# Values of the forgetting heads: three chunks of 344 columns, or two of 512 with half of K in block products

## The chip, the cores and the metric

The kernel runs on one core of one Trainium2 chip. The core's engines each work through a list of instructions of their own: TensorE (PE in the profile, with its weight loads as PEld), VectorE (DVE), ScalarE (ACT), GpSimd (POOL) and SyncE (SP), the last two used here mostly to issue transfers (DMA). The metric is the device time of one execution in microseconds; lower is better.

## The reference

One layer: RMSNorm, one wide projection, two groups of eight attention heads (128 wide), an output projection, and a convolutional feed-forward part, over 256 tokens of width 2048 in float32.

```python
h = rms_norm(x, attn_norm)
proj = h @ w_in                       # 2048 x (3*1024 + 8 + 3*1024)
qa, ka, va, fa, qb, kb, vb = split(proj)
qa, ka = rms_norm(to_heads(qa), q_norm), rms_norm(to_heads(ka), k_norm)
c = cumsum(log_sigmoid(fa + b_forget))         # fa: one column per head, 8 in all
out_a = softmax(qa @ ka.T / sqrt(128) + c[t] - c[s], s <= t) @ va
out_b = stick_breaking(qb, kb, vb)
x = x + concat(rms_norm(out_a), rms_norm(out_b)) @ w_out
x = x + conv_ffn(rms_norm(x))
```

The change concerns `va` (1024 columns) and `fa` (8 columns): `h @ w_in[:, 2048:3080]`.

## The kernel before

**Numbers in two parts.** Each float32 operand of a large product is split into a high part of the type fp32r and the rest, also fp32r: for a weight tile, ScalarE casts (`act.copy`, L220) and VectorE subtracts (L221), both in `split`. A product is then three matmuls: high by high, low tokens by high weights, high tokens by low weights (`in_three`, L237). The tokens `hT` are kept transposed, 16 K tiles of 128 features, each with both parts and 256 tokens; a matmul takes a 128x128 piece of `hT` as the stationary operand and streams the weights' columns.

**A slab.** `token_major` (L253) computes both token tiles for up to 512 columns: for each four K tiles it loads the weights (`load`, three raw buffers), splits them (two buffers each for the high and low parts), and issues 4 x 3 x 2 = 24 matmuls into `acc` (two PSUM banks). After each such slab it calls `step()`, which advances the generators that stand waiting (rows to be normed and transposed, gates, heads), and takes one step of a generator `behind`.

**Order.** The program runs an opening (the first 512 query columns) whose order is written out by hand; behind it PE's order is that of the program and the other engines' order comes from a planner, in which loads and splits have a raised priority. Then come the forgetting heads' values and gates (L558 to L568), the keys' first half, the queries' second half, the keys' second half, the other group, the output projection, and the feed-forward part.

**The values.** Three chunks of 344 columns, 1032 in all, hold the 1024 value columns and the 8 forget columns behind them. `values` scales them by `rstd1` into three tiles: token tile 0 as high and low part, token tile 1 whole.

**Queries and keys.** `fox_rows` (L332) scales a chunk into `raw`, squares it and sums the squares per head on VectorE, takes the root (`rsqrt`, L108: ScalarE's Ln and Exp between short VectorE operations), and multiplies; some steps later it transposes the rows (`ps_h`).

**Block products.** In the output projection half of the columns over half of K already go by a scheme of seven block products in place of eight (`in_seven`, L835): tokens and weights are taken as 2x2 blocks, the tokens' sums are made on VectorE (`block_sums`, `block_parts`), and the weights' sums in place, one on VectorE (`w += x12`) and the others by transfers that add into SBUF on POOL's queue (`plus`). Each product is 12 matmuls of 512 columns into one PSUM bank, and VectorE adds the bank to its targets after each. Products into the same bank accumulate. The scheme's steps are taken by `token_major`, one behind each slab. `pg` (L920), four one-column products, stands in the same stage.

**A transfer near the change.** As soon as `rstd1` is there, POOL writes it to DRAM element by element (`row`, L689) and reads it back as `R1`.

Of the kernel before, what the change touches and what calls it, by code (L numbers as in the profile page):

```python
# [15 lines left out]
P = 128  # L16
D = 2048
S = 256
# [28 lines left out]
def hybrid_layer(  # L47
# [59 lines left out]

    def rsqrt(out_, ss, scale, n):  # L108
# [5 lines left out]
        act.activation(y, y, AF.Exp, scale=-0.5)  # L114
# [3 lines left out]
        dve.tensor_tensor(out_, y, u, op=ALU.mult)  # L118
# [13 lines left out]
    hT = [None] * KT  # L132

    def new_tokens(g):
        t = big.tile([P, 4, 2, S], F32R, name=f"hT{g}", tag=f"hT{g}")
        hT[4 * g : 4 * g + 4] = [t[:, i] for i in range(4)]

# [67 lines left out]
    def load(src):  # L205
        raw = wraw.tile([P, 2048], F32, name="w_raw", tag="w_raw")
        a, b = src.shape[1:]
        nc.sync.dma_start(raw[:, : a * b].rearrange("p (a b) -> p a b", a=a), src)
        return raw

    in_turn, last_split = [], []

    def split(raw, a, b):
        hi = whi.tile([P, 2048], F32R, name="w_hi", tag="w_hi")
        lo = wlo.tile([P, 2048], F32R, name="w_lo", tag="w_lo")
        n = a * b
        with ExitStack() as turn:
            for ins in in_turn:
                turn.enter_context(tc.issue_after(ins.ins))
            last = [act.copy(hi[:, :n], raw[:, :n])]  # L220
            last.append(dve.tensor_tensor(lo[:, :n], raw[:, :n], f32(hi[:, :n]), op=ALU.subtract))  # L221
        last_split[:] = last
        if in_turn:
            in_turn[:] = last
# [79 lines left out]
    with ExitStack() as actx:  # L304
# [9 lines left out]
        def project(c0, cols):  # L314
            return token_major(lambda k: hT[k], wi, 0, KT, c0, cols)
# [15 lines left out]

        def fox_rows(acc, dst, g, steps=2):  # L332
# [6 lines left out]
            for t in range(NT):  # L339
# [3 lines left out]
                dve.tensor_tensor(sq, raw, raw, op=ALU.mult)  # L343
                ss = small.tile([P, 4], F32, name="ss", tag="ss")
                dve.tensor_reduce(ss, sq.rearrange("p (h d) -> p h d", h=4), axis=AX.X, op=ALU.add)
                r = small.tile([P, 4], F32, name="r", tag="r")
                rsqrt(r, ss, 1.0 / HD, 4)
                dve.tensor_tensor(r3, r3, r.unsqueeze(2).to_broadcast([P, 4, HD]), op=ALU.mult)
# [8 lines left out]
        oT_fox = late.tile([P, NH, 2, S], F32R, name="oT_fox")  # L357
        oT = [oT_fox[:, h] for h in range(NH)]
# [4 lines left out]
        def attended(po, h, g, group):  # L363

            if len(done) == NH:
# [175 lines left out]

        qT0 = fox_queries(0)
        waiting.append(fox_rows(acc_q0, qT0, gq, 4))
        step()


        vA_parts = at.tile([P, 2, WF], F32R, name="vA", tag="vA")
        vA = (vA_parts[:, 0], vA_parts[:, 1], vA_rest)
# [8 lines left out]

        lf = at.tile([P, NT, NH], F32, name="lf")  # L558
# [17 lines left out]
        def gates():  # L576
# [4 lines left out]
            act.activation(la, la, AF.Ln, bias=1.0)  # L581
            dve.scalar_tensor_tensor(lf, lf, 0.0, la, op0=ALU.min, op1=ALU.subtract)
# [87 lines left out]
        for half in range(2):  # L670
            if half:
                qT = fox_queries(1)
                waiting.append(fox_rows(project(512, 512), qT, gq, 3))
# [4 lines left out]
            waiting.append(fox_rows(project(WF + 512 * half, 512), kT, g_k))  # L678
# [99 lines left out]
        in_order = tc.keep_in_program_order  # L778
        blocks, sums = [], []

        def block_sums():

            for h, tag in enumerate(("minus_c1", "blocks")):
                blocks.append(at.tile([P, 4, S], F32, name=f"oT_blocks{h}", tag=tag))
# [517 lines left out]
```

## Time and profile before

| | |
|---|---|
| median of 3 runs | 1100.91 us (1100.86 to 1101.10) |
| profiled execution, its own time | 1100.61 us |
| its span, first to last instruction | 1098.8 us |
| granted TensorE clock | 1.000 |
| PE instructions | 5856 matmuls |
| DMA over the span | 249.04 MB, mean 227 GB/s |
| first value slab to first slab of the keys | 31.83 to 78 us |

How to read the lines. The chain of waits in order of time has, for each piece, its start (us), its length (us), the engine, the tile written, the line and the number of instructions. Groups of instructions have the line, engine and operation, output and inputs with their shapes, the count, busy time and the mean of one (ns), and the idle time ahead with what ended it. A window has its bounds and length, then busy time with the count for PE, PEld, DVE, ACT and POOL, the granted clock, the DMA engines' share, and GB/s. Lines on a tile give the shortest, median and longest duration in ns. Lines on transfers have the queue, the count, the size and the median time to landing in us. A wait has who waited for whom, the total in us, how often, and the longest.

### The profile page before, as it was taken

How to read it: one execution, taken by the hardware profiler on the slowest of the kernel's cores; microseconds unless marked ns; L12 is line 12 of the kernel's file. 1: busy time of each engine (PE TensorE's matmuls, PEld its weight loads, DVE VectorE, ACT ScalarE, POOL GpSimd, SP SyncE). 2: the span in 40 equal slices, each digit the busy share in tenths (PEclk: the TensorE clock that was granted, in tenths of full speed). 3: DMA queues.
4: the chain of work that ended last, by engine and by line, in shares of the span. 5: the costliest groups of instructions: out<-in, count | busy, mean ns of one | idle time of the engine just before them, and what ended most of it. 6: DMA issues, size and time to landing. Idle time of an engine off the chain costs nothing.

```text
span 1098.8 us, 14833 instructions
## 1 busy us (share of the span) xinstructions
PE 1094.2 (100%) x5856; PEld 949.3 (86%) x5856; DVE 895.2 (81%) x957; ACT 709.3 (65%) x884; POOL 47.9 (4%) x49
## 2 busy tenths in 40 slices
PE   9999999999999999999999999999999999999998
PEld 7998888888888888888888888888888888888887
DVE  5755777977789776789889988799798889889896
ACT  6544556664665566767757776777676677677753
POOL 0000000000000000001010000100000010100010
PEclk9999999999999999999999999999999999999999
DMA  8776654576639395558999597977979688987985
GB/s 289 183 235 230 190 155 153 192 231 195 226 118 284 110 333 195 168 180 229 278 233 292 191 251 262 259 262 183 320 203 308 211 222 276 248 264 196 324 205 180
DMA packets 180991, 249.04 MB, mean 227 GB/s; under 512 B 4480, under 2 KB 119066, under 8 KB 180666
## 3 DMA queue, kind: packets, MB, share of 16 engines
q1 hardware_dynamic: 162458, 209.67, 58.3%
q0 software_dynamic: 18144, 37.89, 18.4%
q8 instruction: 46, 0.75, 0.3%
q10 hardware_dynamic: 320, 0.53, 0.1%
q14 instruction: 23, 0.19, 0.0%
HBM read 245.97 MB, written 2.11 MB: 226 GB/s over the span
## 4 chain that ended last, share of the span: by engine, by line
PE 100%; ACT 0%; DVE 0%; issue 0%
PE pu L271 34%; PE acc L245 20%; PE pu L277 18%; PE bank_a L245 11%; PE bank_b L245 5%; PE bank_c L245 3%; PE acc L446 2%; PE acc L1180 1%; PE ps_x L146 1%; PE ps_o L612 1%; PE bank_a L1180 1%; PE ps_p L628 0%; PE ps_o L613 0%; PE ps_h L324 0%; PE idle L399 0%; PE ps_s L540 0%
## 5 line engine op out<-in xcount | busy, mean ns | idle before, releaser
L221 DVE TENSOR_TENSOR w_lo<-w_raw,w_hi 128x2048 fp32r<-128x2048 f32 (+1 forms) x194 | 434.9, 2245 | 119.9 <-ACT w_hi L220 119.2
L220 ACT CAST w_hi<-w_raw 128x2048 fp32r<-128x2048 f32 (+1 forms) x194 | 363.6, 1876 | 221.8 <-PE acc L245 61.2
L271 PE MATMUL pu<-hT,w_hi 128*128 128x512 f32 x1664 | 394.0, 390 | 0.0
L271 PEld LDWEIGHTS pu<-hT,w_hi 128*128 128x128 f32 x1664 | 310.3, 188 | 63.1
L277 PEld LDWEIGHTS pu<-hT,w_lo 128*128 128x128 f32 x1664 | 211.9, 191 | 7.0
L277 PE MATMUL pu<-hT,w_lo 128*128 128x256 f32 x1664 | 215.1, 283 | 0.0
L245 PE MATMUL acc<-w_hi,hT 128*128 128x512 f32 (+1 forms) x576 | 124.4, 368 | 0.0
L245 PEld LDWEIGHTS acc<-w_hi,hT 128*128 128x128 f32 x576 | 101.6, 188 | 14.5
L221 DVE TENSOR_TENSOR w_lo<-w_sum,w_hi 128x2048 fp32r<-128x2048 f32 x34 | 77.9, 2290 | 23.1 <-ACT w_hi L220 23.1
L220 ACT CAST w_hi<-w_sum 128x2048 fp32r<-128x2048 f32 x34 | 64.9, 1910 | 46.6 <-PE pu L271 36.4
L997 ACT ACTIVATE tap<-up,ccol 128x256 f32<-128x256 f32 x176 | 74.6, 495 | 0.0
L245 PE MATMUL acc<-w_lo,hT 128*128 128x512 f32 (+1 forms) x288 | 64.6, 366 | 0.0
L245 PEld LDWEIGHTS acc<-w_lo,hT 128*128 128x128 f32 x288 | 51.6, 188 | 7.5
L1102 POOL DMA_DIRECT2D w_sum<-in_w_down_dram x20 | 25.4, 1272 | 678.5 <-DVE w_lo L221 665.4
L245 PE MATMUL bank_a<-w_hi,g 128*128 128x512 f32 x160 | 40.0, 392 | 0.0
L245 PE MATMUL bank_b<-w_hi,s 128*128 128x512 f32 x160 | 40.0, 392 | 0.0
L245 PE MATMUL bank_a<-w_hi,s 128*128 128x512 f32 x160 | 40.0, 392 | 0.0
L245 PEld LDWEIGHTS bank_a<-w_hi,g 128*128 128x128 f32 x160 | 28.9, 189 | 5.3
L245 PEld LDWEIGHTS bank_a<-w_hi,s 128*128 128x128 f32 x160 | 28.9, 189 | 5.3
L245 PEld LDWEIGHTS bank_b<-w_hi,s 128*128 128x128 f32 x160 | 28.9, 189 | 5.3
L1002 DVE TENSOR_TENSOR gate<-gate,tap 128x512 f32<-128x512 f32 x44 | 30.3, 689 | 2.5 <-ACT tap L997 0.2
L1002 DVE TENSOR_TENSOR val<-val,tap 128x512 f32<-128x512 f32 x44 | 30.3, 688 | 2.3
(248 smaller groups left out, 1107.5 us busy)
## 6 DMA issues: line engine op xcount, KB each, us to landing
w_raw<-in_w_up_dram SPq DMA_DIRECT2D x88, 1024.0 KB, 7.6
w_raw<-in_w_down_dram SPq DMA_DIRECT2D x44, 1024.0 KB, 6.0
w_raw<-in_w_in_dram SPq DMA_DIRECT2D x36, 1024.0 KB, 5.5
w_sum<-in_w_down_dram POOLq DMA_DIRECT2D x20, 1024.0 KB, 10.1
w_raw<-in_w_out_dram SPq DMA_DIRECT2D x14, 1024.0 KB, 6.7
w_raw<-in_w_down_dram POOLq DMA_DIRECT2D x10, 1024.0 KB, 14.8
w_raw<-in_w_in_dram SPq DMA_DIRECT2D x12, 688.0 KB, 4.2
w_raw<-in_w_in_dram SPq DMA_DIRECT2D x6, 512.0 KB, 7.0
```

The costliest lines, as they stand in the source:

```text
L146: nc.tensor.transpose(ps[:, j, t * P : (t + 1) * P], xt[t][:, (k + j) * P : (k + j + 1) * P], ident)
L220: last = [act.copy(hi[:, :n], raw[:, :n])]
L221: last.append(dve.tensor_tensor(lo[:, :n], raw[:, :n], f32(hi[:, :n]), op=ALU.subtract))
L245: nc.tensor.matmul(o, lhs(i, l, t), r[:, i, :], start=starts and j == 0, stop=stops and j == 3 * n - 1, skip_group_check=more,)
L271: nc.tensor.matmul(acc[:, j, :], hi[:, i, j * P : (j + 1) * P], hT[k].rearrange("p a b -> p (a b)"), start=k == 0, stop=low_first and k == ...
L277: nc.tensor.matmul(acc[:, j, S:], lo[:, i, j * P : (j + 1) * P], hT[k][:, 0, :], start=False, stop=not low_first and k == KT - 1,)
L446: nc.tensor.matmul(acc[:, t, :], of_half(hT[2 * c + i + j], l, t), r[:, j, :], start=high and c == i == m == 0, stop=not high and c == 7 a ...
L612: nc.tensor.matmul(po, v[j][:, hs], wp[:, k], start=i == 0, stop=False)
L997: act.activation(taps[w][:, j, :], u[:, j, w : w + S], AF.Copy, scale=ccol[:, w, f : f + 1])
L1002: dve.tensor_tensor(a, a, tap, op=ALU.add)
L1102: nc.gpsimd.dma_start(mem[into][:, : nk * 512].rearrange("p (a b) -> p a b", a=nk), src, accum_op=ALU.add)
L1180: nc.tensor.matmul(o, of_half(g, l, t), r[:, i, c0 : c0 + cols], start=kh == 0 and j == 0, stop=kh == n - 1 and j == 11,)
```

## The change

The values become two chunks of 512 columns. For K tiles 8 to 15 they are computed plainly, four slabs. For K tiles 0 to 7 the product is taken by the seven block products, whose code is generalised from the output projection's and used by both; its steps run behind the slabs of the values (one product behind each slab of the second chunk), of the keys' first half and of the queries' second half. The token sums come from `hT`. Each product's bank is added on VectorE, scaled by plus or minus `rstd1`, into four tiles of 512 columns; when all are done, token tile 0 is split into high and low part.

The 8 forget columns are loaded apart (`wg_raw`, 2048 rows of 32 bytes) and multiplied by 64 matmuls: for each K tile and token tile one of 16 columns (high tokens by both weight parts) and one of 8 (low tokens by high weights).

In `fox_rows`, ScalarE squares and sums, head by head, in place of VectorE's product and reduction. The first queries' rows wait three steps in place of four. The splits from the values to the queries' second half are issued in turn, and some behind named instructions (`last_split`): root, squares, rows, gates. `x12`, one tile in the output projection, is two half tiles here. `oT_fox` is allocated when the first head is done, in the buffer that held the token sums.

```diff
 def fox_rows(acc, dst, g, steps=2):
...
-                dve.tensor_tensor(sq, raw, raw, op=ALU.mult)
                 ss = small.tile([P, 4], F32, name="ss", tag="ss")
-                dve.tensor_reduce(ss, sq.rearrange("p (h d) -> p h d", h=4), axis=AX.X, op=ALU.add)
+                for h in range(4):
+                    some = slice(h * HD, (h + 1) * HD)
+                    squared = act.activation(sq[:, some], raw[:, some], AF.Square, accum_out=ss[:, h : h + 1])
+                squares_done.append(squared)
...
+        def in_seven(src, of_tile, sums, w, x12, add, places, idle_steps, prepared, at_once):
+
+            w11, w12, w21, w22 = src
...
+            def product(bank, lhs, parts, to, minus=False):
+                new = bank not in banks
+                if new:
+                    pool, tag = places[bank]
+                    banks[bank] = pool.tile([P, 512], F32, name=bank, tag=tag)
+                in_three([banks[bank]], parts, 4, lhs, new, True, more=not new)
+                add(*to, banks[bank], minus)
...
+            for _ in range(idle_steps):
+                yield
+            if not at_once:
+                first_loads(moved, (w, w11))
+            product("bank_a", of_blocks(0, 0), prepared(lambda: split(w, 4, 512), sum_weights), (0, 0))
+            if not at_once:
+                yield
+                first_loads(moved_x12, (w12,))
+            product("bank_c", of_blocks(1, 0), weights(w21, 4, 512), (0, 0))
+            yield
+            if not at_once:
+                last_split.append(gates_done[0])
+                with tc.issue_after(gates_done[-1].ins):
+                    sum_weights()
+                yield
+                last_split.extend(gates_done)
+            parts = split_ahead(w)
+            moved(nc.gpsimd, w, w22, accum_op=ALU.add)
+            moved_x12(nc.gpsimd, w22, accum_op=ALU.add)
+            product("bank_b", of_sums(0, 1), parts, (1, 1))
+            yield
+            product("bank_b", of_sums(1, 0), weights(w22, 4, 512), (0, 1))
+            yield
+            parts = split_ahead(w)
+            moved(nc.gpsimd, w, w21, accum_op=ALU.add)
+            product("bank_a", of_sums(1, 1), parts, (0, 1), True)
+            yield
+            product("bank_a", of_sums(0, 0), split_ahead(x12), (1, 1), True)
+            yield
+            product("bank_a", of_blocks(1, 1), split_ahead(w), (1, 0))
...
+        def values_in_seven():
+
+            sums = late.tile([P, 2, NH, S], F32R, name="hT_sums", tag="eight")
+            last_split.append(rooted_done[0][1])
+            with tc.issue_after(rows_done[-1].ins):
+                block_parts(block_sums(hT_of_four[:2]), [sums[:, part] for part in range(2)])
+
+            def add(t, h, ps, minus=False):
+                some = value_columns[t][h]
+                factor = (minus_rstd1 if minus else rstd1)[:, t : t + 1]
+                dve.scalar_tensor_tensor(some, ps, factor, some, op0=ALU.mult, op1=ALU.add)
...
+        nc.sync.dma_start(wg_raw, rows_of(wi, 0, KT, 3 * WF, NH))
+        act.copy(wg[:, :, 0, :], wg_raw)
+        dve.tensor_tensor(wg[:, :, 1, :], wg_raw, f32(wg[:, :, 0, :]), op=ALU.subtract)
+        ordered[0] = True
+        last_split.clear()
+        seven = values_in_seven()
+        for h in range(2):
+            if h:
+                last_split.append(squares_done[-1])
+            acc = token_major(lambda k: hT[8 + k], wi, 8, 8, 2 * WF + 512 * h, 512, seven)
+            for t in range(NT):
+                scaled(value_columns[t][h], acc[:, t, :], t)
+
         lf = at.tile([P, NT, NH], F32, name="lf")
-        for j in range(3):
-            acc = project(2 * WF + 344 * j, 344)
-            n = 344 if j < 2 else 336
+        pf = psb.tile([P, NT, 2, NH], F32, name="pf", tag="t")
+        for k in range(KT):
             for t in range(NT):
-                if j == 2:
-                    dve.scalar_tensor_tensor(
-                        lf[:, t, :], acc[:, t, 336:344], rstd1[:, t : t + 1], bf,
-                        op0=ALU.mult, op1=ALU.add,
-                    )
-            values([v[:, 344 * j : 344 * j + n] for v in vA], acc[:, :, :n])
+                nc.tensor.matmul(
+                    pf[:, t].rearrange("p a h -> p (a h)"), of_half(hT[k], 0, t),
+                    wg[:, k].rearrange("p a h -> p (a h)"), start=k == t == 0, stop=False,
+                )
+                nc.tensor.matmul(
+                    pf[:, t, 0, :], of_half(hT[k], 1, t), wg[:, k, 0, :], start=False, stop=k == KT - 1 and t == NT - 1,
+                )
...
-                waiting.append(fox_rows(project(512, 512), qT, gq, 3))
+                waiting.append(fox_rows(project(512, 512, seven), qT, gq, 3))
+                ordered[0] = False
...
-            waiting.append(fox_rows(project(WF + 512 * half, 512), kT, g_k))
+            waiting.append(fox_rows(project(WF + 512 * half, 512, seven), kT, g_k))
```

More of the change, by code (lines that the diff above doesn't have):

```diff
@@ L353, in fox_rows @@
             yield
-        oT_fox = late.tile([P, NH, 2, S], F32R, name="oT_fox")
-        oT = [oT_fox[:, h] for h in range(NH)]
+        oT, oT_fox = [], []
         vA_rest = late.tile([P, WF], F32, name="vA_rest", tag="two_heads")
@@ L363, in attended @@
         def attended(po, h, g, group):
+            if not done:
+                oT_fox.append(late.tile([P, NH, 2, S], F32R, name="oT_fox", tag="eight"))
+                oT.extend(oT_fox[0][:, h] for h in range(NH))
             if len(done) == NH:
```

226 lines of the change are left out of this document (127 added, 99 removed).

## The prediction

> **What bounds the kernel now.** I read the page first, then what TensorE (PE) waited for, then the chain of waits in order of time around the values, then the same chain around the output projection, where the block scheme already runs.
>
> ```profile
> PE 1094.2 (100%) x5856; PEld 949.3 (86%) x5856; DVE 895.2 (81%) x957; ACT 709.3 (65%) x884; POOL 47.9 (4%) x49
> PE 100%; ACT 0%; DVE 0%; issue 0%
> ...
> PE idle L399 <- DVE zeros L389: 1.1, 1, 1.1
> PE acc L446 <- ACT hT L151: 0.3, 1, 0.3
> ```
>
> PE is busy over the whole span, the chain is all PE, and in the whole run it waited twice, for 1.4 us, both at the start. So the time is the sum of PE's instructions. An edit gains what it takes from PE, loses what it adds there, and everything on the other engines is free until PE has to wait for it.
>
> ```profile
> 31.83 15.12 PE acc L245 x96
> 46.95 0.87 PE ps_h L324 x8
> 47.82 35.73 PE acc L245 x216
> ...
> 83.76 5.47 PE acc L245 x24
> ```
>
> The values are 3 chunks of 344 columns by four slabs (a slab is one load of weights, four K tiles) of 24 matmuls, 288 in all. The first four slabs (x96) take 15.12 us, 3.78 each. The 216 matmuls behind them hold eight such slabs and the first slab of the keys (5.47, as its successor): (35.73 - 5.47) / 8 = 3.78. **Removed from PE: 12 x 3.78 = 45.4 us.**
>
> **What takes its place on PE.** Two kinds are shown at full size by the output projection:
>
> ```profile
> 307.22 5.44 PE acc L245 x24
> 312.66 0.34 PE pg L920 x4
> 313.00 5.61 PE acc L245 x24
> ...
> 325.92 2.75 PE bank_a L245 x12
> 328.67 2.72 PE bank_c L245 x12
> ```
>
> The second half of K, plain: 2 chunks x 2 slabs = 4 slabs of 24 matmuls of 512 columns, 4 x 5.44 = 21.8 us. The first half of K: seven products of 12 matmuls, 7 x 2.73 = 19.1 us. Together 40.9 us, that is 4.5 less than was removed (the columns streamed fall from 288 x 344 = 99,072 to 180 x 512 = 92,160).
>
> The third kind is new: 16 K tiles x 2 token tiles x 2 parts = 64 matmuls that stream 16 or 8 columns, each with its own 128x128 stationary tile of `hT`. The streaming is nearly nothing; each still needs its weight load. The nearest rows are the four one-column products `pg`, which also load a full 128x128 tile each:
>
> ```profile
> L920 PEld LDWEIGHTS pg<-cs,ssq x8: 187/190/192, 312.3 to 347.8; 128*128 128x128 f32 x8
> L920 PE MATMUL pg<-cs,ssq x8: 164/250/250, 312.5 to 347.8; 128*128 128x1 f32 x8
> ...
> L245 PEld LDWEIGHTS acc<-w_hi,hT 128*128 128x128 f32 x576 | 101.6, 188 | 14.5
> ```
>
> On the chain four of them cost 0.34 us, 0.085 each; but the slab behind them takes 5.61 in place of 5.44, since its first load is exposed too: (0.34 + 0.17) / 4 = 0.128 each. These are my bounds: 64 x 0.085 = 5.4 and 64 x 0.128 = 8.2 us. In a run of 64 the ends (one load hidden before, one exposed behind) count for little, so I take the value between, 0.110: **64 x 0.110 = 7.0 us added**. A load is 188 ns long for tiles of `hT` and 190 for `ssq`; that the type (fp32r here, fp32 in `pg`) makes it cheaper is not to be seen; 344- or 512-column products hide such a load behind the product before, 16 columns hide none of it.
>
> The Trainium skill speaks against that price: "TensorE: Matmul & The Clock Gate", section "Back-to-back issue gap", gives a floor of about 25 ns for matmuls of 1 to 64 columns; that is the first rival below. The same page, "LDWEIGHTS (loading the stationary operand)", gives columns / 1.2 ns, 107 ns for 128; the trace agrees with that one (0.085 to 0.128).
>
> Sum on PE: -45.4 + 21.8 + 19.1 + 7.0 = **+2.5 us**; with the bounds +0.9 to +3.7. Against the profiled execution's 1100.61 us this is 1103.1; the median of the runs shown is 0.3 above that execution, so 1103.4.
>
> **What is added beside PE, costed at nothing.** These five windows reach from the first value slab to the second slab of the next queries:
>
> ```profile
> 31.80:47.60 15.80, 15.80 (x106) 15.78 (x104) 11.39 (x24) 6.56 (x12) 1.84 (x3) 1.00 0.79 151
> 47.60:62.80 15.20, 15.20 (x100) 15.20 (x98) 7.57 (x6) 8.50 (x9) 0.00 (x0) 1.00 0.83 251
> 62.80:77.90 15.10, 15.10 (x98) 15.10 (x98) 7.56 (x5) 6.83 (x7) 0.00 (x0) 1.00 0.75 249
> 77.90:99.70 21.80, 21.80 (x98) 17.66 (x98) 10.78 (x10) 9.31 (x11) 1.59 (x3) 1.00 0.74 242
> 99.70:122.70 23.00, 23.00 (x112) 19.28 (x111) 17.55 (x30) 10.69 (x16) 0.00 (x0) 1.00 0.60 193
> ...
> L221 DVE TENSOR_TENSOR w_lo<-w_raw,w_hi 128x2048 fp32r<-128x2048 f32 x10 | 22.9, 2292 | 17.4 <-ACT w_hi L220 17.4
> L221 DVE TENSOR_TENSOR w_lo<-w_raw,w_hi 128x1376 fp32r<-128x1376 f32 x12 | 19.1, 1590 | 15.9 <-ACT w_hi L220 15.9
> L343 DVE TENSOR_TENSOR sq<-raw 128x512 f32<-128x512 f32 x4 | 2.6, 686 | 0.0
> L345 DVE TENSOR_REDUCE ss<-sq 128x4 f32<-128x512 f32 x4 | 2.5, 680 | 0.0
> ...
> L786 DVE TENSOR_TENSOR oT_blocks<-oT_fox 128x1024 f32<-128x1024 f32 x2 | 2.4, 1220 | 0.0
> L833 DVE SCALAR_TENSOR_TENSOR x<-bank_b,rg,x 128x512 f32<-128x512 f32 x2 | 1.5, 750 | 0.3 <-PE bank_b L245 0.3
> ...
> w_sum<-in_w_out_dram POOLq DMA_DIRECT2D x2, 1024.0 KB, 10.4
> ```
>
> VectorE (the third number after the span) is busy 54.9 of 90.9 us there. Twelve splits of 1.59 go (-19.1), eleven of 2.29 come (+25.2: four plain, seven for the products); the weights' sum 2.3, block sums (2 x 1.22 and four of about 0.69) 5.2, their low parts 2.4, seven bank reads of 0.75 5.3; squares and reductions leave for ScalarE (-5.1); the values' own low parts about even. That is 71 of 93.4 us, 76%: it fits, and so does ScalarE by the like sum (41.9 to some 59 us, squares included). The cover is the same slab of PE work that hides a split today: two splits (4.6 us on VectorE) against a slab and a product (5.44 + 2.72 = 8.2). Without it a split costs its 2.29 us on PE. The chain of three in-place sums of `w` through POOL's queue, 10.4 us to land in the output projection (last row above), has 11 us and more between the split before and the product behind; `minus_c`'s transfers stand in that queue too, but are short. Three waits are new on the queues: the third slab's cast on ScalarE stands behind the eight squares, `w_11`'s behind the queries' root, the sum of weights on VectorE behind the gates. PE is the only one that waits for these splits. The new `wg_raw` load waits for no buffer, so on SP it can go ahead of the second value slab's weights, which do.
>
> **Rivals.**
>
> *The small products are cheap* (ends faster).
>
> ```profile
> 312.50 0.28 PE L920 MATMUL pg<-cs,ssq 128*128 128x1 f32 x2
> ```
>
> The first two `pg` take 0.28 us together and the second 0.25 by itself (its median above): it starts 0.03 us behind the first, so its load was done ahead. If every load of `hT` could overlap its neighbour like that, the 64 would cost 64 x 0.03 = 1.9 us: 1100.6 - 4.5 + 1.9 = 1098.0. It decides from 4.5 / 64 = 70 ns down. Against it: the four `pg` together average 85, so the third and fourth had to wait for their loads. The Trainium skill's floor, above, would be an estimated 64 x 0.025 = 1.6 us here and 1097.7.
>
> *A transfer comes late at the start* (slower still).
>
> ```profile
> 26.50:30.00 3.50, 3.50 (x16) 2.64 (x15) 2.50 (x5) 3.50 (x6) 0.00 (x0) 1.00 0.00 0
> 37.50:46.00 8.50, 8.50 (x56) 8.50 (x56) 7.48 (x18) 3.24 (x6) 0.54 (x1) 1.00 0.67 29
> 46.00:52.00 6.00, 6.00 (x42) 5.98 (x42) 2.08 (x3) 3.46 (x6) 0.00 (x0) 1.00 0.97 311
> ACT w_hi L220: 5.3, 1
> DMA to landing us min/median/max: 4.2/4.5/11.1
> DMA packets 308, 0.15 MB, mean 128 GB/s; under 512 B 171, under 2 KB 308, under 8 KB 308
> ```
>
> Each window's last number is GB/s: from 37.5 to 46.0 us the transfers move 29 while `rstd1` is written to DRAM element by element; a slab's load took 11.1 us and ScalarE waited 5.3 us for it, without reaching PE. After the change, PE wants the first product's cast (`w_11`) at 31.8 + 3 x 5.44 = 48.2, so its load by 46.3; the fourth slab by 49.0, `w_21` by 54.4. Ahead of these the queue has two slabs a third larger, and `wg_raw`: 2048 packets of 32 bytes, 128 an engine. In the window where the forget bias's 128 packets of that size pass (22.2 to 23.4), 308 packets take 1.2 us, 62 ns each on an engine: 8 us for `wg_raw`, of which the 3.5 us without a transfer before 30.0 us cover less than half. If `w_11` has all its 1 MB left at 46.0, it lands at 49.4 (3.4 us at 311 GB/s) and PE waits 3.1 us; the fourth slab and `w_21`, each 3.4 us behind the one before, add 0.7 and 1.4: 5.2 in all, 1108.3. With half of it left, about half: 1106. By my count PE's loads just make it.
>
> *The third slab's cast is late.*
>
> ```profile
> 35.62 1.26 ACT L318 ACTIVATE raw<-acc,rstd 128x512 f32<-128x512 f32 x2
> ...
> L658 ACT ACTIVATE pr<-pr,nm 128x128 f32<-128x128 f32 x1 | 0.4, 402 | 4.2 <-DVE nm L655 4.2
> L658 ACT ACTIVATION_READ_ACCUMULATOR pr<-pr,nm 128x1 f32 x1 | 0.2, 187 | 0.0
> L220 ACT CAST w_hi<-w_raw 128x2048 fp32r<-128x2048 f32 x10 | 19.1, 1912 | 21.6 <-PE acc L245 21.5
> ```
>
> `raw` is scaled by 36.9 us, or 0.9 sooner now that the third cast (34.4 to 35.7 before) goes behind it. Eight squares of 128 columns take at most 8 x 0.59 (0.40 + 0.19, as this accumulating activation), to 40.7; the cast of 1.91 ends at 42.6, and PE wants it at 31.8 + 2 x 5.44 = 42.7. A slip of 1 us gives 1104.4.
>
> **How the numbers follow.** Forecast, no new wait on PE and small products at 0.110 us: 0.55, 1103.4. Late transfer: 0.20, 1106. Late cast: 0.13, 1104.4. Cheap small products: 0.07, 1098.0 to 1100. Something else: 0.05. The range 1101.5 to 1107.5 runs from the lower bound of the small products (+0.9) to most of the late transfer. What can be told from no change is 0.2%, 2.2 us: the forecast lies only just beyond it, and a small product of 0.105 us or less falls back into it, so of its 0.55 some 0.09 count as the same. Slower 0.83, same 0.10, faster 0.07.
>
> **What would show it.** Four plain slabs at 5.44 and seven products at 2.72 on the chain; one piece of 64 small matmuls, 7.0 us long, between the last `bank_c` and the keys; PE's waits still those two. Wrong if that piece is below 4.5 us, or if PE waits for `w_hi` between 42 and 57 us by more than 1 us.

## The result, and the profile after

The changed kernel takes 1112.79 us, median of 5 executions (1111.2 to 1114.0), against 1101.1 (1100.86 to 1102.04) for the kernel before: a ratio of 1.0104 with a 95% interval of 1.0089 to 1.0118. The sign was forecast, the size was not: the 11.7 us are nearly five times the 2.5 of the forecast, and the time lies beyond its range of 1101.5 to 1107.5. The profiled execution took 1114.0 us, 13.4 more than that of before, its span is 1112.2 us and its mean granted clock (the share of full speed at which PE was let run) 0.994 in place of 1.000.

First the page's row on the engines and the waits of PE, for the changed kernel.

```profile
PE 1103.4 (99%) x5812; PEld 950.2 (85%) x5812; DVE 908.0 (82%) x961; ACT 725.3 (65%) x951; POOL 52.8 (5%) x53
...
PE ps_o L789 <- DVE pT L810: 2.6, 1, 2.6
PE acc L463 <- ACT w_hi L453: 1.5, 1, 1.5
...
```

PE has 44 matmuls fewer and is busy 9.2 us longer, and two waits of over a microsecond are new: 1.5 us in the opening, and 2.6 us for a tile of the heads (`pT`), a hundred microseconds behind the values. Neither stands where the prediction had looked. The chain around the values, in order of time (start, length, tile):

```profile
33.72 16.34 PE acc L254 x72
...
50.93 2.73 PE bank_a L254 x12
53.67 5.44 PE acc L254 x24
59.11 2.72 PE bank_c L254 x12
61.83 0.01 PE pf L732
61.84 0.11 PE pf L736
...
66.08 0.11 PE pf L736
...
66.30 0.20 PE pf L736
...
71.00 0.21 PE pf L736
71.20 8.10 PE acc L254 x24
```

The first slab starts 1.9 us late; from there up to 61.83 all is as forecast: four slabs of 5.44 (16.34 is three of them), products of 2.72. The small products start at their forecast price too: the L736 ones from 61.84 to 66.08 are 19 pairs in 4.24 us, 0.112 a product. Then, from 66.30 on, each takes twice as long, and the keys' first slab behind them, also busy throughout, takes 8.10 us in place of 5.44 to 5.47. The windows over that stretch, and one later on, say why (bounds, length, busy time with count of PE, PEld, DVE, ACT and POOL, granted clock, DMA share, GB/s):

```profile
61.80:66.20 4.40, 4.40 (x43) 4.40 (x41) 2.22 (x3) 1.99 (x2) 0.00 (x0) 1.00 0.74 242
66.20:71.20 5.00, 5.00 (x25) 5.00 (x25) 0.00 (x0) 0.00 (x0) 0.00 (x0) 0.50 0.10 36
71.20:76.40 5.20, 5.20 (x14) 4.04 (x14) 5.09 (x8) 0.65 (x3) 0.56 (x1) 0.50 0.14 24
...
168.60:172.00 3.40, 3.08 (x14) 3.08 (x15) 1.95 (x5) 1.24 (x3) 0.00 (x0) 0.50 0.66 179
```

4.4 us after the row began, the granted clock fell to 0.50 and stayed there for 10.2 us, through the rest of the row and most of the slab behind it. PE waited for nothing: it is busy 5.00 of 5.00 us. The row took 71.20 - 61.83 = 9.37 us in place of 7.0, the slab 2.6 too much: **5.0 us** that no instruction and no wait accounts for. The Trainium skill has the two states and a free-running window of about 3.4 us in "TensorE: Matmul & The Clock Gate", section "What's actually happening"; the trace agrees (0.50 and 1.00, and 10.2 us is three such windows). Its section "HAM oscillation" ties the fall to waits for transfers, and here there was none.

The opening, on ScalarE's timeline (idle time ahead and what ended it in brackets):

```profile
25.49 0.30 ACT L716 CAST wg<-wg_raw 128x128 fp32r<-128x128 f32 x1 [3.42 <-DMA wg_raw<-in_w_in_dram]
...
26.42 1.04 ACT L453 CAST w_hi<-w_raw 128x1024 fp32r<-128x1024 f32 x1
```

The cast of the forget weights stands between two pieces of the opening and waits 3.42 us for its transfer. Behind it stand the transposed tokens and a cast that PE wants; the first value slab starts at 33.72 in place of 31.83: **1.9 us**.

The heads, on the chain of waits of the changed kernel (`ps_o` is a head's output, `pT` its transposed probabilities, `pu` a projection's products, taken between):

```profile
165.65 0.36 PE ps_o L789 x3
...
166.25 2.28 DVE w_lo L232
168.53 0.35 DVE pT L810
...
168.92 0.80 PE ps_o L789 x2
...
170.14 2.78 PE pu L286 x16
```

and the same place before:

```profile
156.39 0.36 PE ps_o L612 x3
...
157.56 1.91 PE pu L277 x16
```

A head's second product now waits for `pT`, which stands on VectorE behind a split; and after that gap the clock fell once more, for 3.4 us from 168.6 (the last of the windows above), so that `pu` takes 2.78 in place of 1.91. On ScalarE the cause stands ahead of it:

```profile
160.67 0.30 ACT L357 ACTIVATE sq<-raw 128x128 f32<-128x128 f32 x1
...
163.17 0.19 ACT L357 ACTIVATION_READ_ACCUMULATOR sq<-raw 128x1 f32 x1
163.27 0.35 ACT L808 CAST pT<-ps_p 128x256 fp32r<-128x256 f32 x1
```

Eight squares of the keys' second half run for 2.7 us, and the heads' casts wait behind them. From the first `ps_o` to the end of `pu` is (170.14 + 2.78) - 165.65 = 7.27 us, before 157.56 + 1.91 - 156.39 = 3.08: **4.2 us**.

With the balance of 2.5 forecast: 1.9 + 2.5 + 5.0 + 4.2 = 13.6, and 13.4 were measured.

### The profile page after: what moved, and what is told of

Same layout as the page of the kernel before. It is cut to its first block, busy times and chain, and to the rows that moved or that the text cites. A ratio compares the mean times of both kernels' runs of the same rounds, so it can differ in the third digit from the quotient of the medians.

```text
span 1112.2 us, 14814 instructions
## 1 busy us (share of the span) xinstructions
PE 1103.4 (99%) x5812; PEld 950.2 (85%) x5812; DVE 908.0 (82%) x961; ACT 725.3 (65%) x951; POOL 52.8 (5%) x53
## 4 chain that ended last, share of the span: by engine, by line
PE 97%; DVE 0%; issue 0%
PE pu L280 34%; PE pu L286 18%; PE acc L254 18%; PE bank_a L254 12%; PE bank_b L254 6%; PE bank_c L254 3%; PE acc L1291 1%; PE ps_o L789 1%; PE acc L463 1%; PE bank_a L1291 1%; PE ps_p L805 0%; PE pf L732 0%; PE pf L736 0%; PE ps_o L790 0%; PE ps_x L149 0%; PE ps_h L333 0%
## 5 line engine op out<-in xcount | busy, mean ns | idle before, releaser
L232 DVE TENSOR_TENSOR w_lo<-w_raw,w_hi 128x2048 fp32r<-128x2048 f32 x188 | 429.6, 2289 | 101.9 <-ACT w_hi L229 99.2
L229 ACT CAST w_hi<-w_raw 128x2048 fp32r<-128x2048 f32 x188 | 358.8, 1911 | 197.2 <-PE pu L280 54.9
L254 PE MATMUL acc<-w_hi,hT 128*128 128x512 f32 x448 | 109.5, 398 | 0.0
L229 ACT CAST w_hi<-w_sum 128x2048 fp32r<-128x2048 f32 x38 | 72.6, 1909 | 52.5 <-PE pu L280 35.7
L232 DVE TENSOR_TENSOR w_lo<-w_sum,w_hi 128x2048 fp32r<-128x2048 f32 x38 | 87.0, 2289 | 21.6 <-ACT w_hi L229 21.6
L254 PEld LDWEIGHTS acc<-w_hi,hT 128*128 128x128 f32 x448 | 85.1, 192 | 17.5
L254 PE MATMUL acc<-w_lo,hT 128*128 128x512 f32 x224 | 55.4, 389 | 0.0
L254 PEld LDWEIGHTS acc<-w_lo,hT 128*128 128x128 f32 x224 | 42.0, 188 | 8.8
L1101 ACT ACTIVATE gate<-up,ccol 128x256 f32<-128x256 f32 x44 | 24.1, 595 | 14.1 <-DVE up L1094 9.2
```

The lines of the kernel that those rows point to most:

```text
L229: copied = act.copy(hi[:, some], r[:, :m])
L232: rest = dve.tensor_tensor(lo[:, some], r[:, :m], f32(hi[:, some]), op=ALU.subtract)
L254: nc.tensor.matmul(o, lhs(i, l, t), r[:, i, :], start=starts and j == 0, stop=stops and j == 3 * n - 1, skip_group_check=more,)
L1101: act.activation(a[:, j, :], u[:, j, 2:], AF.Identity, scale=ccol[:, 2, f : f + 1], bias=ccol[:, 3, f : f + 1],)
```

## The experiments

The theory after this reading: the balance of PE is right, and three separate things came on top: the clock, the opening, the squares. The rival was that these are three faces of one cause, or that the clock falls for a reason of its own. The first three sets of runs put each part alone into the kernel before, or take it out of the changed one.

**The small products alone, in the kernel before.** Behind the last value slab 64 products of the same shapes are added, whose sums nothing uses; all else is as before. In the second run they are four groups of 16, one behind each of the last chunk's four slabs.

```diff
+                        nc.tensor.matmul(
+                            extra[:, t].rearrange("p a h -> p (a h)"), of_half(hT[k], 0, t), hT[k][:, 0, :16],
+                            start=k == t == 0, stop=False,
+                        )
+                        nc.tensor.matmul(
+                            extra[:, t, 0, :], of_half(hT[k], 1, t), hT[k][:, 0, :8], start=False,
...
+                yield
```

> The kernel before with 64 small products added in one row, behind its last value slab (16 or 8 columns of the tokens against 128x128 pieces of the tokens; the result is read and not used). Theory (half clock after a long row of small products): 7.1 us for the row at full clock, and the clock at 0.5 for some 7 to 10 us that begin 3 to 7 us into the row: 10 to 12.5 us more, 1111 to 1113.5. Rival (only the weight loads count): 7.1 us more, 1108.2, and the clock at 1.0.

> The kernel before with the same 64 small products in four groups of 16, one behind each of the last four value slabs. Theory (the clock falls only when a stretch of some 3.4 us holds little but small products): 7.1 us more, 1108.2, the clock at 1.0. Rival (any small products bring the clock down, or their price is not their weight load): the same as in one row, over 1110, or under 1105.

The row gave 1113.33 us (1111.87 to 1115.45; ratio 1.0112, 1.0096 to 1.0129), the groups 1108.38 (1107.91 to 1108.54; 1.0066, 1.0051 to 1.0081). Windows of the row's run, and one of the groups':

```profile
78.60:82.90 4.30, 4.30 (x41) 4.30 (x39) 3.13 (x4) 2.19 (x6) 0.00 (x0) 1.00 0.79 251
82.90:88.20 5.30, 5.30 (x27) 5.30 (x26) 0.00 (x0) 0.00 (x0) 0.00 (x0) 0.50 0.60 195
88.20:93.10 4.90, 4.90 (x12) 3.84 (x13) 0.26 (x2) 0.00 (x0) 0.00 (x0) 0.50 0.00 0
```

```profile
60.00:90.00 30.00, 30.00 (x201) 29.11 (x200) 11.61 (x12) 11.40 (x13) 0.00 (x0) 1.00 0.58 185
```

The same fall, 4.3 us into the row and 10.2 us long, with PE and its weight loads busy all through the row, in a kernel that has nothing else of the change; cut in four, the same 64 products leave the clock at 1.00. The 4.95 us between the two runs are the clock's price (less up to 1.1 us, a wait of PE in the opening that the row's profile has and the groups' has not), the 7.4 between the groups and before (1108.38 - 1100.99) the products': the forecast of 7.0 was right for that alone.

**Two rows of 32.**

> The kernel before with the same 64 small products as two rows of 32, one behind the last value slab and one behind the product that follows it. One row of 64 gave 1113.3 us with half clock for 10.2 us, four of 16 gave 1108.4 without. Theory (the clock falls when a stretch of about 3.4 us, at a place that the row does not choose, has little but small products): a row of 3.5 us fills such a stretch only by chance, so no half clock or one step of 3.4 us in some executions: 1108 to 1110. Rival (any row longer than the 1.7 us of a group is enough): half clock behind both rows, 1112 us or more. Rival (the clock counts the sum of small products, not their order): as the row of 64, 1113.

The rows stand behind the third and the fourth slab of the last value chunk: a slab of 344 columns follows the first row, and the keys' first slab, of 512, the second. The median was 1111.75 us (ratio 1.0100, 1.0080 to 1.0121). The four executions took 1109.83, 1109.94, 1113.56 and 1114.65 us, with mean clocks of 0.998, 0.998, 0.995 and 0.994. The profiled one (1109.94), the window behind the first row and the one behind the second:

```profile
78.60:82.00 3.40, 3.40 (x14) 3.40 (x13) 0.00 (x0) 0.00 (x0) 0.00 (x0) 0.51 0.91 289
...
87.00:90.40 3.40, 3.40 (x16) 2.83 (x17) 0.39 (x3) 0.00 (x0) 0.00 (x0) 1.00 0.75 227
```

The first row was followed by one step of 3.4 us at half clock, the second, as long, by none. So neither the length of a row alone nor the sum of the products decides. The falls last 3.4 and 10.2 us here, and 13.6 in a run below, one, three and four times the same step; that it matters how much of such a step a row fills, and that the steps lie elsewhere in each execution, would fit, but it is not shown, and the columns of the slab behind the row differ too. The median came out over the 1108 to 1110 expected, since two of the four executions lost more.

**The squares alone, in the kernel before, and taken out of the changed kernel.**

```diff
-                dve.tensor_tensor(sq, raw, raw, op=ALU.mult)
-                dve.tensor_reduce(ss, sq.rearrange("p (h d) -> p h d", h=4), axis=AX.X, op=ALU.add)
+                for h in range(4):
+                    some = slice(h * HD, (h + 1) * HD)
+                    act.activation(sq[:, some], raw[:, some], AF.Square, accum_out=ss[:, h : h + 1])
```

> The kernel before with the squares of the rows on ScalarE, as the change has them, and nothing else. Theory (these squares alone hold up the heads' casts): PE waits some 2.6 us behind the second key half, and 1 to 4 us are lost, 1102 to 1105. Rival (it takes the block products beside them): PE waits for nothing new and the time stays within 0.3 us of the kernel before.

> The changed kernel with the squares and their sums of the rows back on VectorE, as before the change. Theory (eight squares on ScalarE hold up the casts of a head's weights behind the second key half, PE waits 2.6 us for them at 166 us and its clock then halves for 3.4 us): that wait and that half clock go, the time falls by about 4 us, to about 1109. Rival (the wait comes from the heads' place against the splits, which the block products moved): the wait stays, and VectorE's added work makes it no shorter: no change or slower.

In the kernel before, the squares on ScalarE cost 4.5 us: 1105.49 (1103.36 to 1105.85; ratio 1.0034, 1.0021 to 1.0047). Two of its five executions, with a mean clock of 1.000, took 1103.36 and 1103.74 us; three, with 0.998, 1105.49 to 1105.85. By these, the wait by itself costs about 2.6 us, and the fall of the clock, which does not come every time, some 2 more. The profiled execution is one of the three; its wait:

```profile
PE ps_o L613 <- DVE pT L634: 2.5, 1, 2.5
```

The chain of that run shows the whole path: ScalarE is late with `pT`, hence with the cast of the weights, VectorE's split waits for that cast, and the other `pT` for the split.

```profile
155.50 1.81 ACT w_hi L220
...
157.33 2.29 DVE w_lo L221
159.62 0.34 DVE pT L634
...
160.01 0.51 PE ps_o L613 x2
```

With the squares back on VectorE the changed kernel takes 1109.99 us (1109.05 to 1112.92; ratio 1.0079, 1.0062 to 1.0096). The wait for `pT` and the fall of the clock behind it are gone; the opening's wait stays (1.4 us), and the clock fell in the row once more, here for longer:

```profile
64.90:78.50 13.60, 13.60 (x53) 12.44 (x53) 5.30 (x8) 0.65 (x3) 0.77 (x1) 0.50 0.26 80
```

Four steps of 3.4 us in place of three: in this execution, the slowest of the four, the clock ate part of the gain of 4.2. The median fell by 2.8 only. The mean clocks of the four executions, 0.994 to 0.997, are those of the changed kernel, though the fall behind `pT` is gone; a longer fall in the row would explain that, but only this one execution shows it.

**The cast of the forget weights behind the opening.**

```diff
-        act.copy(wg[:, :, 0, :], wg_raw)
-        dve.tensor_tensor(wg[:, :, 1, :], wg_raw, f32(wg[:, :, 0, :]), op=ALU.subtract)
+        with tc.issue_after(rooted_done[0][0].ins), tc.issue_after(rooted_done[0][1].ins):
+            act.copy(wg[:, :, 0, :], wg_raw)
+            dve.tensor_tensor(wg[:, :, 1, :], wg_raw, f32(wg[:, :, 0, :]), op=ALU.subtract)
```

> The changed kernel with one edit: the cast and the subtraction of the forget columns' weights stand behind the first root on ScalarE and VectorE, out of the opening. Theory (in the changed kernel ScalarE waited 3.4 us for their load inside the opening, PE 1.5 us behind it): the wait of PE in the opening goes, the first value slab starts at about 31.9 us in place of 33.7, and the time falls by 1.8 us, to about 1111. Rival (the late opening is scatter of one execution): the first value slab starts where it did, between 31.8 and 33.7, with no wait for these weights moved, and the median stays within 0.5 us.

1112.39 us (1109.68 to 1114.22; ratio 1.0102, 1.0084 to 1.0119): by the median no gain that can be told. The part that was meant did happen: on PE's timeline the first value slab, with its first instruction's start in the first column, comes at

```profile
31.73 3.79 PE L254 MATMUL acc<-w_hi,hT 128*128 128x512 f32 x16
```

against 33.56 in the changed kernel in the same view, and the opening's wait is gone. The four executions lie at 1109.68, 1111.48, 1113.31 and 1114.22 us with mean clocks of 0.997, 0.995, 0.994 and 0.992. A stretch of t us at half clock lowers the mean by 0.5 t / 1110, so these are by estimate about 7, 11, 13 and 18 us at half clock, the fall behind `pT` among them: the clock differs by more, from one execution to the next, than the edit is worth. Whether the opening's 1.9 us reach the end can therefore be judged only without the row's fall, in the run with all three costs taken away, below.

**The small products in groups, in the changed kernel.** Four groups of 16, one behind each value slab, ahead of the product that stands there.

```diff
+        def gates_and_seven():
+            for g in range(4):
+                for k in range(4 * g, 4 * g + 4):
...
+                next(seven, None)
+                yield
...
-            acc = token_major(lambda k: hT[8 + k], wi, 8, 8, 2 * WF + 512 * h, 512, seven)
+            acc = token_major(lambda k: hT[8 + k], wi, 8, 8, 2 * WF + 512 * h, 512, both)
```

> The changed kernel with the 64 small products in four groups of 16, one behind each value slab, in place of one row of 64. Theory (a long row of small products lets PE's granted clock fall to half, from 66.2 to 76.4 us, and that cost 2.3 us in the row and 2.7 us in the slab behind it): each group takes 1.8 us, 0.111 each, the clock stays at 1.0 there, and the time falls by about 5 us, to about 1108. Rival (the small products are slow by themselves, 9.4 us for 64, and the slab behind them waits for something else): the groups take 2.3 us each and the time stays within 1 us.

1110.23 us (1108.95 to 1110.40; ratio 1.0081, 1.0066 to 1.0096). No fall of the clock among the values, the waits of the opening and for `pT` as in the changed kernel. From the parts measured so far, 1100.8 - 4.5 + 7.4 + 1.9 + 4.2 = 1109.8.

**All three at once.** First as the three edits just shown, unchanged:

> The changed kernel with all three edits: the cast out of the opening, four groups of small products, squares on VectorE. Theory (the three costs stand apart, 1.8 + 5 + 4 of the 13.4 us by which the profiled execution was longer): what is left is PE's own balance, -45.4 + 40.9 + 7.1 = +2.6 us over the kernel before, 1103.5. Rival (the stage has another cost that shows when these are gone, or they overlap): over 1105.

1111.61 us (1111.04 to 1112.00; ratio 1.0096, 1.0081 to 1.0111). The expectation fell, and the waits of PE show by what:

```profile
PE pf L727 <- ACT rs_y L115: 4.1, 1, 4.1
```

The first group, behind the first slab, now needs a cast that was put behind the root. PE stood for 4.1 us, and the windows over the wait and behind it:

```profile
36.00:40.40 4.40, 1.48 (x7) 0.90 (x5) 4.40 (x7) 1.62 (x1) 0.00 (x0) 1.00 1.42 351
40.40:50.60 10.20, 9.03 (x29) 7.87 (x30) 8.06 (x20) 0.54 (x4) 0.55 (x1) 0.50 0.81 182
```

The clock fell during the wait and stayed at half for 10.2 us, with the first group of small products right behind the wait, so how much of that is the gap's doing is not told apart here. Two edits that each did their part collided: against the run below, where they don't, the wait of 4.1 us and the fall cost 1111.61 - 1104.01 = 7.6 us.

Then with the groups one place later: behind the second, third and fourth slab, and the last group behind the products.

```diff
+            for g in range(4):
+                if g:
+                    gate_products(g - 1)
+                next(seven, None)
+                yield
...
+        gate_products(3)
```

> The changed kernel with all three extra costs taken away and none added: the 64 small products in four groups of 16 (three behind the second, third and fourth value slab, one behind the last block product), the cast of the forget weights behind the last piece of the root, the squares on VectorE. Theory (three separate causes beside the balance of PE): no wait of PE over 0.5 us in the opening or the heads, no granted clock of 0.5. PE's balance is -45.4+21.8+19.1 = -4.5 without the small products, and the four groups cost 7.3 us where they stood alone in the kernel before (span 1098.8 to 1106.1): +2.8, so 1103.8 us, between 1103 and 1105. Rival (the causes are one: whatever is changed, something else becomes late for the same sum): 1108 us or more with a new wait of PE, as in the first try at all three. Rival (a cost of the changed kernel that has not been seen, spread over PE): 1106 to 1107.5 with no wait and no half clock.

1104.01 us (1103.60 to 1104.80, 7 executions; ratio 1.0029, 1.0017 to 1.0040), within 0.3 us of what was expected, and both rivals fall. Its waits of PE, and its span and mean granted clock:

```profile
PE idle L415 <- DVE zeros L405: 1.1, 1, 1.1
PE bank_a L254 <- DVE x L1203: 0.2, 1, 0.2
```

```profile
core 0: 1102.2 us, clock 1.000
```

With the three causes taken away and none put in, 3.1 us remain: the balance of PE, forecast at 2.5.

**Without the small products.** The gates are made from 16 columns of the last value slab's sums instead, so the forget columns aren't computed.

```diff
-            dve.scalar_tensor_tensor(lf[:, t, :], pf[:, t, 1, :], factor, bf, op0=ALU.mult, op1=ALU.add)
+            dve.scalar_tensor_tensor(lf[:, t, :], acc[:, t, 0:8], factor, bf, op0=ALU.mult, op1=ALU.add)
```

> The changed kernel without the 64 small products: the gates are made from the first 16 columns of the last value slab's sums in place of the forget columns, so the output is not the reference's. Theory (row and half clock together cost 7.1 + 5): 12 us less than the changed kernel, about 1100.8. Rival (no half clock, weight loads alone): 7 us less, about 1105.8.

1109.57 us (1109.23 to 1109.86; ratio 1.0077, 1.0062 to 1.0092): a miss. The row is gone and its fall of the clock with it, but the chain has a new stretch:

```profile
78.52 13.61 DMA w_sum<-in_w_in_dram
...
92.23 1.91 ACT w_hi L229
...
94.18 5.31 PE bank_a L254 x12
```

The in-place sum of weights, in POOL's queue behind the gates, lands late; PE waits 4.2 us for its cast, and the product behind takes 5.31 in place of 2.72. Here the gap has only wide products behind it, and the clock was at 0.50 from about 92.4 to 99.2 us, 6.8 us, two steps. The balance of PE, the opening, the heads, this wait and this product add up: -4.5 + 1.9 + 4.2 + 4.2 + 2.6 = 8.4 of the 8.6 us measured over before. Without the row, PE wants this product 11.8 us earlier (90.0 in place of 101.75), while the transfer is issued only 4.3 us earlier (78.52 in place of 82.8): the row had given it time. But it also took 13.6 us to land, in place of at most 8.8 in the changed kernel; with 8.8 its cast would have been done at 89.2, just in time. Why it took longer was not looked into.

**The operands swapped.** The late cast and the squares on VectorE as above; the forget columns as 16 products whose stationary operand is the 16 weight columns and whose moving operand is 512 columns of tokens, both parts at once, in one row behind the second slab. Two small fp32 products then add the parts and turn them to tokens.

```diff
+            for k in range(KT):
+                nc.tensor.matmul(
+                    pf[: 2 * NH].rearrange("p a s -> p (a s)"), wg[:, k].rearrange("p a h -> p (a h)"),
+                    hT[k].rearrange("p a s -> p (a s)"), start=k == 0, stop=k == KT - 1,
+                )
...
+        both_parts = at.tile([2 * NH, NH], F32, name="both_parts")
...
+            nc.tensor.matmul(
+                pg_t[:, t, :], fsum[:, t * P : (t + 1) * P], both_parts, start=t == 0, stop=t == NT - 1
+            )
```

> As the run with the late cast and the squares on VectorE, but the forget columns as 16 products whose stationary operand is the 16 weight columns and whose moving operand is the 512 columns of both halves of the activations, in one row behind the second value slab; two small fp32 products then add the parts and turn them to tokens. Theory (small products cost what they do because each pays for a load of 128 columns of activations and streams 16 or 8): 16 x 0.227 = 3.6 us in place of 7.0, the clock stays at 1.0 because 512 columns stream, and the balance is -4.5+3.6+0.2 = -0.7: 1100.4 us, between 1099.8 and 1101.5, the same as before. Rival (only 16 of 128 columns of the array are used, so these products count as idle too): half clock for 3.4 us or more after the row, 1102 to 1105. Rival (the sum in place of the late transfer is no longer hidden, as without the small products): a wait of PE for w_hi of 1 to 4 us at 90 us, 1104 to 1109.

1107.11 us (1106.48 to 1107.38; ratio 1.0055, 1.0040 to 1.0070). The row does what was expected, and the clock stays at 1.00, but the slabs around it are slower. On the chain:

```profile
43.45 3.70 PE pf L731 x16
47.16 5.60 PE acc L254 x24
```

The slabs take 5.60 in place of 5.44, with no new wait of PE. One thing that the run had added beside the products is `both_parts`, 32 bytes a partition in a pool of SBUF, with the weight tiles behind it. So the next run makes that tile 64 bytes, the one after puts it into the tile of the raw forget weights, where it adds nothing, and the last adds such a tile to the kernel before and leaves it unread:

```diff
+        pad = at.tile([P, NH], F32, name="pad")
+        dve.memset(pad, 0.0)
```

> The run before it (operands swapped) with the new little tile of 32 bytes a partition made 64 bytes, and nothing else. There every 512-column product took 232 ns in place of 227, from the opening on, long before the first changed instruction, until about 400 us, some 1,000 to 1,700 products. Theory (the tile of 32 bytes moved the weight tiles behind it in SBUF off a multiple of 64 bytes, and products that read them stream 2.3% slower): 227 ns again all through, and the balance as worked out there, 1100.4 us, between 1099.8 and 1101.5. Rival (something of the swapped products themselves, their output of 16 rows or the two fp32 products, or more traffic on SBUF, slows the stage): 232 ns again and 1106.5 to 1107.5 us.

> The swapped kernel with the little matrix that adds the parts written into the tile of the raw forget weights, which is free by then, so that no tile of SBUF is added. Theory (the tiles' place sets the rate): 227 ns for 512-column products as in the kernel before, 1.2 us less than with 64 bytes (5.44 in place of 5.50 a slab, and the same share of the 1,500 products up to 400 us: about 2), so 1100.6 us, between 1099.9 and 1101.3: the same as before or just under it. Rival (the swapped products or the added traffic cost the rest): 229 ns and 1102.4 to 1103.2.

> The kernel before with one tile of 32 bytes a partition more among those of the attention stage, set to zero and never read: the weight tiles behind it lie 32 bytes further on. Theory (the tiles' place sets the rate): 232 ns in place of 227 for 512-column products up to about 400 us, as in the swapped kernel with the 32-byte tile, and 5 to 8 us: 1106 to 1109. Rival (the place has nothing to do with it): 227 ns and 1100.9 us, within 0.5.

With 64 bytes: 1102.74 us (1102.35 to 1103.67; ratio 1.0016, 1.0007 to 1.0025), slabs of 5.50, so that run fell between its two cases, and a tile of 64 bytes does not bring the rate back in full. Without an added tile: 1101.22 (1100.65 to 1101.76; ratio 1.0003, 0.9994 to 1.0012). Its chain from the second slab's end:

```profile
42.81 3.71 PE pf L731 x16
...
55.61 5.44 PE acc L254 x24
```

And the kernel before with the unread tile: 1105.43 (1105.12 to 1105.73; ratio 1.0041, 1.0028 to 1.0053), its only wait of PE the 1.1 us at the start. The keys' first slab is the last of the row of 216, their second the one behind it, which took 5.47 before:

```profile
48.34 35.73 PE acc L245 x216
...
84.29 5.58 PE acc L245 x24
```

An unread tile of 32 bytes costs 4.5 us, a little less than the 5 to 8 expected. Most slabs of 512 columns up to some 400 us take about 2% more; slabs of 344 columns don't: with 5.58 for the slab of the keys, the eight in the row of 216 take (35.73 - 5.58) / 8 = 3.77 each, before 3.78. The edit changes only the place of the tiles behind and adds one setting to zero at the start, where PE waits no longer than before. So the place in SBUF is the cause as far as these runs go; which tile, and what about its address, was not tried.

## Why the prediction was wrong

**The balance of PE** was right. Slabs of 5.44 and products of 2.72 stand on the chain as forecast, the small products cost 0.112 each against 0.110, and the kernel with the extra costs taken away stands 3.1 us over before where 2.5 was forecast. The bounds of 0.085 and 0.128 held. That 0.110 came so near is partly luck, since it was picked between the bounds; and that 16 columns hide none of a load is not what the row shows: its loads are 187 to 192 ns long at full clock, so at 0.112 us a product one load overlaps the next. The floor of about 25 ns that the prediction set against its price is not reached by products that each have a load of their own. The group of 16 with the load that lies bare behind it costs 1.85 us (7.4 / 4), 0.115 a product.

**The step that failed first** is "64 x 0.110 = 7.0 us added": a price an instruction, taken at a granted clock of 1.00, was multiplied by 64 as if the clock didn't depend on what PE runs; the forecast has no term for the clock. `pg`, the row it came from, has four products between slabs; sixteen in a group behave like it, 64 in a row don't. The two runs in the kernel before price what was missed at 3.9 to 4.95 us; in the changed kernel 2.4 us of it lie in the row and 2.6 in the slab behind it. The forecast's own test, "one piece of 64 small matmuls 7.0 us long", gave 9.37.

**The second** is "What is added beside PE, costed at nothing". Squares were moved to ScalarE with the argument that ScalarE's total fits. It does: 725.3 us of 1112.2. But a queue is served in order, and the rival of the late cast looked at one place only, the first eight squares. That one went well (three slabs in 16.34 us). The same eight squares recur in the keys' second half just ahead of a head's casts, with a cast of weights and its split behind them on the way to PE: 4.5 us alone in the kernel before, with a fall of the clock, by their mean clocks, in three of five executions.

**The third** is the cast of the forget weights, which the working did not place at all. It was counted as queue time for `wg_raw` on SP; what cost 1.9 us was ScalarE's place for the cast, in the opening, ahead of instructions that PE needs, and a wait of 3.42 us in it.

**The rivals.** The late transfer, held the likeliest of them, didn't come: PE waited for no `w_hi` between 42 and 57 us. Another transfer did come 4.2 us late, in the run without the small products: the in-place sum, to which the prediction gave 11 us and more of room; from its issue to the product that wants it there were 90.0 - 78.5 = 11.5 us, a cast of 1.9 included, and it took 13.6 to land. The small products weren't cheap. The late third cast did not happen there, but its mechanism, squares ahead of a cast, did elsewhere.

**The sign** was right for a reason that the experiments bear out: with the three extra costs out, the kernel is still slower by the forecast's own sum (1.0029, 1.0017 to 1.0040). One thing in the change decides that, the forget columns' own products. With their operands swapped and the other two costs removed, the kernel stands at 1101.22, not told from before (1.0003, 0.9994 to 1.0012): the 4.5 us that the block products save pay for 3.7 us of swapped products and 0.54 us of the two behind them, and little is left. No version that was run beats the kernel before.

## What to carry to other kernels

A row of matmuls that stream few columns is priced per instruction and by the clock that it leaves behind: here groups of 1.8 us between wide products left the clock at 1.00 and rows of 3.5 us did so only at times; with the operands swapped, so that the wide one streams, a row of 3.7 us left it there too. An engine's free time says nothing of an instruction's place in its queue: for each instruction moved, look at every recurrence of it and at what stands right behind, down to PE. A wait of PE of some 2.5 us or more is to be priced with the half clock that can follow it; the wait of 1.5 us in the opening brought none. A changed kernel that is slower all through, with no wait, may have had its tiles shifted.

## What was not expected of the hardware

- The granted clock fell to 0.50 while PE and its loads were busy without a gap, in products of 16 and 8 columns, 2.9 to 4.4 us after the start of a row of 64, for about 10.2 us in three profiles and 13.6 in one. Swapped products, which use 16 of the stationary operand's columns and stream 512, left it at 1.00.
- A gap of 2.6 us (`pT`) was followed by half clock for 3.4 us; one of 4.2 us with wide products behind it brought 6.8 us, from 2.4 us into the gap on, and one of 4.1 us with 16 small products behind it 10.2 us. One of 1.5 us in the opening left the clock at 1.00.
- 2048 packets of 32 bytes, which the prediction put at 8 us, landed 4.7 us after they were issued.
- 32 bytes more in SBUF ahead of the weight tiles made most slabs of 512-column products up to some 400 us 5.58 to 5.60 us long in place of 5.44 to 5.47; 64 bytes made them 5.50; slabs of 344 columns took no longer.
